# Gate weights of a gated linear recurrence get buffers of their own, gate blocks move between the recurrence's groups, and the last norm is reordered

## Chip, cores and metric

One core of one Trainium2 chip runs the whole layer in one launch. The metric is the device time of the launch in microseconds, the median of several runs. Engines are named as in the profile: PE is TensorE (PEld its weight loads), DVE is VectorE, ACT is ScalarE, POOL is GpSimd, SP is SyncE, which here issues nearly all DMAs.

## The reference, cut to what matters

The layer takes x of 256 tokens by 2048 and runs a half-step feed-forward with a norm, a mixer of two parallel branches with a norm, and a second feed-forward with a norm:

```python
h = layer_norm(DN_ALPHA * h + 0.5 * swiglu(h, ffn1_w_in, ffn1_w_out), ln1_g, ln1_b)
q, k, v, qi, ki, wi, rx, rg, gates = split_cols(h @ w_in)
y_attn = dsa_attention(q, k, v, qi, ki, wi)          # attention over the selected keys
# recurrent branch: 2560 channels in 16 blocks of 160
xc = causal_conv(rx, conv_w) + conv_b                # 4 taps
r  = sigmoid(blockdiag(xc, wa) + ba);  i = sigmoid(blockdiag(xc, wx) + bx)
a  = exp(-8 * r * softplus(-lam));     b = sqrt(1 - a*a) * (i * xc)
y_rnn = scan(h_t = a_t * h_{t-1} + b_t) * gelu(rg)
g_attn, g_rnn = split(sigmoid(gates))
merged = g_attn * (y_attn @ w_attn_branch) + g_rnn * (y_rnn @ w_rnn_branch)
h = layer_norm(DN_ALPHA * h + merged @ w_out, ln2_g, ln2_b)
h = layer_norm(DN_ALPHA * h + 0.5 * swiglu(h, ffn2_w_in, ffn2_w_out), ln3_g, ln3_b)
```

All data are float32.

## The kernel before, in words

**Products in parts.** Every float32 operand of a product is split into a high part (a rounded copy, made by ACT) and a low part (the difference, made by DVE). A product is three matmuls: high by high, low by high, high by low. For the weights the two halves of the split are the tiles `wh` (ACT, L203) and `wl` (DVE, L204), written from `raw`, the tile into which SP's DMA puts the weights.

**One stream of weights.** A list of pieces of at most 1024 columns is laid down once, in the order in which PE will use them. When PE's code comes to a new piece (`W.unit`), the load of the piece eight further is issued and the split of the piece four further. There are 4 buffers for `raw` and 5 for each of `wh` and `wl`, whatever the size of a piece. So the `raw` buffer of a new load is one whose piece DVE has just split, and the `wh`/`wl` buffer of that split is one whose piece PE has just finished.

**Order on the engines.** PE, SP and POOL run in the order in which the program is written. DVE and ACT are ordered by a scheduler at compile time, mostly by the order of writing; on the chip each engine then takes its instructions strictly in that order.

**The recurrent stage** is a loop over j from 0 to 21 (`NR` = 20 tiles of 128 channels, `LAG` = 2). For j below 20 two blocks (`blockB`, L594 and L595) project x and the gelu input of tile j; DVE and ACT sum the parts, run the convolution (L1297) and split the result into `xc`. Then, for tile i = j - 2, the gate products use 256 columns of the block-diagonal weights `lru`: `corners` for the first tile of a group, `squares` for the others (`L1247`), and `lru_gates` follows with four ACT operations (L1264 to L1267) and a reciprocal on DVE (L1268). The 20 tiles form four groups of five. At a group's last tile (i = 4, 9, 14, 19, so j = 6, 11, 16, 21) PE also runs `squares` for the group's first tile and 16 narrow matmuls (`strips`, L1254) on the weights `lx`; after that a background task `recur` does the group's square roots, products and scan, a few instructions at each new piece of the stream. `bg.drain("rec")` emits what is left of it.

**Gate blocks.** `gates(nb)`, nb = 0 to 3, multiplies x by 512 columns of the branch's output gate `wG`: 8 pieces, 96 matmuls of 512 columns, with two ACT operations (`gr`, L1278) at its end and no other work for DVE than the split of its weights. Before the change gates(0) stands at the start of j = 20, gates(1) to gates(3) after the loop. The weights `lru` are small pieces of the common stream (24 of them, 256 columns each); `lx` is loaded twice, for two groups at a time.

**The last norm** (`OuterNorm.product`, `norm`, `turned`) ends the kernel. The tokens are two halves, t = 0 and 1. For each, when the last product is in PSUM: statistics (L865, L756, L757) on DVE, the power of -0.5 on POOL (L758), then on DVE three column blocks are centred (L871) and scaled (L879) with a DMA out after each (L880), and the small factor `nm` (L875) is made for the fourth block, which ACT scales (L876), PE transposes (L887), ACT scales again (L891) and SP writes out (L892).

## Time and profile before

| what | value |
|---|---|
| median of 3 runs | 2260.11 us (2259.5 to 2261.3) |
| the profiled execution | 2260.29 us |
| its span in the profile | 2258.2 us |
| PE busy | 2236.4 us (99%) |
| DVE busy | 1956.0 us (87%) |
| ACT busy | 1445.1 us (64%) |
| recurrent stage (loop over j) | from 1061.7 to about 1321 us |
| gates(0), j = 20 | 1295.8 to 1317.9 us |
| end of the last product on PE | about 2247.7 us |

The span starts at the first instruction and ends at the last one; the profiled execution's own time has 2.1 us around it. In a row of the timeline the columns are start, duration, engine, line, operation, tiles; a bracket at the end gives the idle time of the engine before it and what ended it. A matmul of 512 columns is shown with 0.38 us, but in an unbroken row the next starts 0.22 us later, so matmuls overlap in such rows and a PE shown as busy may still have lost a little.

### The profile page before, as it was taken

The numbers are of one execution on the slowest core, as the hardware profiler recorded it, in microseconds if no ns is written. First come the engines' busy times: TensorE is split into PE (matmuls) and PEld (weight loads), VectorE is DVE, ScalarE is ACT, GpSimd is POOL, SyncE is SP. The second block draws the span as 40 slices with busy tenths as digits, with TensorE's granted clock in tenths as the row PEclk, the third lists the DMA queues.
The fourth block names the chain that finished last, engine by engine and source line by source line (L and its number), as shares of the span: only waits on it lengthen the run. The fifth ranks groups of instructions, "written<-read, shape, count | busy, mean of one in ns | idle before, by whom it ended". The sixth has DMA issues, their size and how long they took to land.

```text
span 2258.2 us, 34888 instructions
## 1 busy us (share of the span) xinstructions
PE 2236.4 (99%) x13328; PEld 2023.3 (90%) x13328; DVE 1956.0 (87%) x2743; ACT 1445.1 (64%) x2062; POOL 19.8 (1%) x54
## 2 busy tenths in 40 slices
PE   9999999999999999999999999999999999999998
PEld 8999999999988888888998888888899999999997
DVE  7999999999998776645799985656999999999997
ACT  6667777667756555544677774444766777777664
POOL 0000000000000000000000000000000000000000
PEclk9999999999999999999999999999999999999999
DMA  8555566555567655566555567666665555566554
GB/s 319 199 205 191 217 224 224 210 210 207 198 194 222 181 174 153 164 198 208 178 188 184 188 217 214 192 202 191 220 209 214 204 200 197 216 224 233 215 206 149
DMA packets 114760, 459.57 MB, mean 204 GB/s; under 512 B 12929, under 2 KB 16257, under 8 KB 100257
## 3 DMA queue, kind: packets, MB, share of 16 engines
q1 hardware_dynamic: 112176, 450.41, 59.0%
q0 software_dynamic: 1840, 5.89, 0.9%
q8 instruction: 104, 1.70, 0.3%
q10 hardware_dynamic: 576, 1.05, 0.1%
q14 instruction: 64, 0.52, 0.1%
HBM read 455.20 MB, written 2.10 MB: 203 GB/s over the span
## 4 chain that ended last, share of the span: by engine, by line
PE 87%; DVE 9%; issue 2%; ACT 1%; DMA 1%; POOL 0%; POOLq 0%; ACTq 0%; DVEq 0%
PE mm L605 11%; PE mm L607 11%; PE mm L606 11%; PE ob L605 10%; PE ob L607 10%; PE ob L606 10%; PE bp L606 4%; PE bp L607 4%; PE bp L605 4%; DVE wl L204 4%; PE mm L594 2%; PE ob L594 2%; PE mm L595 1%; PE ob L595 1%; PE bp L958 1%
## 5 line engine op out<-in xcount | busy, mean ns | idle before, releaser
L204 DVE TENSOR_TENSOR wl<-raw,wh 128x1024 fp32r<-128x1024 f32 (+2 forms) x644 | 759.8, 1185 | 239.4 <-ACT wh L203 237.1
L203 ACT ACTIVATE wh<-raw 128x1024 fp32r<-128x1024 f32 (+2 forms) x644 | 658.7, 1028 | 356.5 <-PE ob L607 138.6
L203 ACT ACTIVATE wh<-rf 128x1024 fp32r<-128x1024 f32 x336 | 301.8, 917 | 140.9 <-PE mm L607 84.9
L204 DVE TENSOR_TENSOR wl<-rf,wh 128x1024 fp32r<-128x1024 f32 x336 | 346.0, 1039 | 2.4
L605 PE MATMUL mm<-wh,hs 128*128 128x512 f32 (+1 forms) x704 | 247.3, 351 | 0.3 <-ACT hs L796 0.2
L607 PE MATMUL mm<-wh,hs 128*128 128x512 f32 (+1 forms) x704 | 244.0, 347 | 1.5 <-DVE hs L797 1.3
L605 PE MATMUL ob<-wh,g 128*128 128x512 f32 x640 | 245.5, 384 | 0.0
L606 PE MATMUL mm<-wl,hs 128*128 128x512 f32 (+1 forms) x704 | 243.6, 346 | 0.7 <-DVE wl L204 0.7
L607 PE MATMUL ob<-wh,g 128*128 128x512 f32 x640 | 242.7, 379 | 0.5 <-DVE g L737 0.5
L606 PE MATMUL ob<-wl,g 128*128 128x512 f32 x640 | 242.6, 379 | 0.0
L605 PE MATMUL bp<-wh,sh 128*128 128x256 f32 x672 | 185.0, 275 | 0.0
L606 PE MATMUL bp<-wl,sh 128*128 128x256 f32 x672 | 184.9, 275 | 0.0
L607 PE MATMUL bp<-wh,sl 128*128 128x256 f32 x672 | 184.8, 275 | 0.0
L203 ACT ACTIVATE wh<-ws 128x1024 fp32r<-128x1024 f32 x112 | 119.2, 1064 | 81.4 <-issue 52.7
L607 PEld LDWEIGHTS mm<-wh,hs 128*128 128x128 f32 x704 | 133.7, 190 | 16.1 <-DVE hs L797 3.2
L605 PE MATMUL mm<-wh,xs 128*128 128x512 f32 (+1 forms) x448 | 146.8, 328 | 0.8 <-ACT wh L203 0.8
L606 PE MATMUL mm<-wl,xs 128*128 128x512 f32 (+1 forms) x448 | 146.8, 328 | 0.5 <-DVE wl L204 0.5
L605 PEld LDWEIGHTS mm<-wh,hs 128*128 128x128 f32 x704 | 133.7, 190 | 14.7 <-issue 1.0
L607 PE MATMUL mm<-wh,xs 128*128 128x512 f32 (+1 forms) x448 | 146.5, 327 | 0.0
L606 PEld LDWEIGHTS mm<-wl,hs 128*128 128x128 f32 x704 | 133.8, 190 | 13.2 <-DVE wl L204 1.0
L176 DVE TENSOR_TENSOR ws<-rf 128x1024 f32<-128x1024 f32 x112 | 136.4, 1218 | 4.4 <-DMA rf<-f1a 2.1
L607 PEld LDWEIGHTS ob<-wh,g 128*128 128x128 f32 x640 | 121.0, 189 | 18.0 <-DVE g L737 0.9
(335 smaller groups left out, 5131.7 us busy)
## 6 DMA issues: line engine op xcount, KB each, us to landing
rf<-f1a SPq DMA_DIRECT2D x56, 1024.0 KB, 5.0
rf<-f2a SPq DMA_DIRECT2D x56, 1024.0 KB, 5.1
raw<-f1o SPq DMA_DIRECT2D x88, 512.0 KB, 5.8
raw<-f2o SPq DMA_DIRECT2D x88, 512.0 KB, 5.9
raw<-wB SPq DMA_DIRECT2D x80, 512.0 KB, 3.8
raw<-wA SPq DMA_DIRECT2D x64, 512.0 KB, 3.6
raw<-wG SPq DMA_DIRECT2D x64, 512.0 KB, 3.7
raw<-f2a SPq DMA_DIRECT2D x64, 512.0 KB, 4.6
```

The lines of the kernel that those rows point to most:

```text
L176: v.tensor_tensor(t, b[:, 0:4:3], b[:, 1:2].to_broadcast([P, 2, 2, 256]), op=OP.add)
L203: nc.scalar.activation(hp, src, AF.Copy)
L204: self.last = nc.vector.tensor_tensor(lp, src, hp, op=OP.subtract)
L594: T.matmul(ps, w[0], turns(x.rearrange("p a t -> p (a t)")), start=first, stop=False)
L595: T.matmul(ps[:, :S], w[1], turns(x[:, 0]), start=False, stop=last)
L605: T.matmul(ps, xh, h, start=start, stop=False, skip_group_check=seeded)
L606: T.matmul(ps, xh, l, start=False, stop=False, skip_group_check=seeded)
L607: T.matmul(ps, xl, h, start=False, stop=stop, skip_group_check=seeded)
L958: T.transpose(ps[:, k * S + t * P:k * S + (t + 1) * P], z[:, t * 512 + k * P:t * 512 + (k + 1) * P], ident)
```

## The change

Four edits:

- **Gate weights.** The 24 pieces of `lru` leave the common stream. A new `load_gates(i)`, called at the start of step j = i + 2, ahead of that step's two blocks where there are any, issues a DMA into a small tile `lr` and splits it into a tile `lw` of its own (ACT L733, DVE L734; line numbers of the new kernel differ from those before by up to three). Same products, same sizes.
- **`lx`** is loaded four times, once per group, into a small tile, instead of twice into a large one.
- **Gate blocks.** gates(0) goes to the start of j = 12, gates(1) to the start of j = 17, gates(2) to the start of j = 20, gates(3) after the loop.
- **Last norm.** `nm` moves from DVE to POOL; two blocks are centred before the first is scaled; and 14 products of the 128x128 identity with itself stand on PE between the transposes of t = 0 and those of t = 1.

```diff
+GR_AT = (12, 17, NR)
+WARM_END = 14
...
-    for i in range(NR + LAG):
+    for i in range(NR + 1):
+        if i in GR_AT:
+            plain([wG[4 + GR_AT.index(i)]])
         if i < NR:
             plain([wB[RX + i], wB[RG + i]])
-        if i == NR:
-            plain([wG[4]])
-        if i >= LAG:
-            g, c = divmod(i - LAG, TPG)
-            plain([lru[g][:, c * 2 * P:(c + 1) * 2 * P]])
-            if c == TPG - 1:
-                plain([lru[g][:, TPG * 2 * P:]])
-    plain(wG[4 + nb] for nb in range(1, 4))
+    plain([wG[7]])
...
                 self.turned(0)
+                warm = BP()
+                for _ in range(WARM_END):
+                    T.matmul(warm[:, :P], ident, ident, start=True, stop=True)
                 self.norm(1, ps[1], rows)
...
+            nm = SM(1)
+            G.tensor_scalar(nm, mu, r, -1.0, op0=OP.mult, op1=OP.mult)
             centered(0)
-            nm = SM(1)
-            V.tensor_scalar(nm, mu, r, -1.0, op0=OP.mult, op1=OP.mult)
+            centered(1)
             A.activation(Y[t][3], ps, AF.Identity, scale=r, bias=nm)
             for nb in range(3):
...
-                if nb < 2:
-                    centered(nb + 1)
+                if nb == 0:
+                    centered(2)
...
+    def load_gates(i):
+        g, c = divmod(i, TPG)
+        for c in (c,) if c < TPG - 1 else (c, TPG):
+            raw, hl = T1("lr"), UHL("lw")
+            nc.sync.dma_start(raw, lru[g][:, c * 2 * P:(c + 1) * 2 * P])
+            split(hl, raw)
+            lw.append([(hl[:, 0, o:o + P], hl[:, 1, o:o + P]) for o in (0, P)])
...
     for j in range(NR + LAG):
-        if j == NR:
-            gates(0)
-        if j < NR and j % (2 * TPG) == 0:
-            lx = QG("lx")
-            nc.sync.dma_start(lx, lru_x[j // (2 * TPG)])
-            lxs += [lx[:, :2 * P], lx[:, 2 * P:]]
+        if j in GR_AT:
+            gates(GR_AT.index(j))
+        if j % TPG == LAG and j < NR:
+            lxs.append(T1("lx"))
+            nc.sync.dma_start(lxs[-1], lru_x[j // TPG])
+        if j >= LAG:
+            load_gates(j - LAG)
...
-    for nb in range(1, 4):
-        gates(nb)
+    gates(3)
     hs = None
     bg.drain("rec")
```

`corners` and `squares` take their weights from `lw` instead of from the stream; nothing else in them changes.

**PE at the end of the second group (from j = 11 to 12).** The last strip matmul of the group and what follows, before:

```order
L1254 MATMUL bp_12462<-xg_12121,lx_10883 32x256
L594 MATMUL mm_12491<-hs_7425,wh_12397 128x512
L595 MATMUL mm_12491<-hs_7425,wl_12398 128x256
L594 MATMUL mm_12491<-hs_7426,wh_12397 128x512
L595 MATMUL mm_12491<-hs_7426,wl_12398 128x256
```

The same place after the change:

```order
L1254 MATMUL bp_12456<-xg_12114,lx_11762 32x256
L602 MATMUL mm_12479<-wh_12340,hs_7425 128x512
L603 MATMUL mm_12479<-wl_12341,hs_7425 128x512
L604 MATMUL mm_12479<-wh_12340,hs_7425 128x512
L602 MATMUL mm_12479<-wh_12340,hs_7426 128x512
```

Where the next block of j = 12 stood, gates(0) now begins (L602 to L604 are the three matmuls of such a block, L605 to L607 before), and the blocks of j = 12 come 96 matmuls later.

**SP around j = 20.** The DMAs of the last `lru` weights (the tiles of i = 18, of i = 19, and those of the last group's first tile) among the loads of the gate weights, before:

```order
L161 DMA raw_13599<-wG 128x1024
L161 DMA raw_13629<-wG 128x1024
L161 DMA raw_13652<-lru 128x256
L161 DMA raw_13673<-lru 128x256
L161 DMA raw_13691<-lru 128x256
L161 DMA raw_13709<-wG 128x1024
```

And after (`raw_14064` is the last piece of gates(3), whose load is issued when PE's code comes to the last piece of gates(2)):

```order
L163 DMA raw_14046<-wG 128x1024
L163 DMA raw_14064<-wG 128x1024
L1284 DMA lr_14086<-lru 128x256
L1284 DMA lr_14105<-lru 128x256
L1284 DMA lr_14110<-lru 128x256
L163 DMA raw_14153<-wrb 128x1024
```

Before, the three loads stood right behind the eight pieces of the gates(0) that PE runs ahead of them, and ahead of the eight of the next block; now they stand behind all eight of the next block.

**DVE around j = 20.** The splits of those weights, before:

```order
L204 TENSOR_TENSOR wl_13712<-raw_13629,wh_13711 128x1024
L204 TENSOR_TENSOR wl_13730<-raw_13652,wh_13729 128x256
L204 TENSOR_TENSOR wl_13748<-raw_13673,wh_13747 128x256
L204 TENSOR_TENSOR wl_13766<-raw_13691,wh_13765 128x256
L204 TENSOR_TENSOR wl_13784<-raw_13709,wh_13783 128x1024
```

And after (`wl_14067` is the fourth piece of gates(3), `wl_14156` the fifth; `vw_14097` belongs to tile i = 18):

```order
L206 TENSOR_TENSOR wl_14067<-raw_13992,wh_14066 128x1024
L206 TENSOR_TENSOR wl_14156<-raw_14010,wh_14155 128x1024
L734 TENSOR_TENSOR lw_14087<-lr_14086,lw_14087 128x256
L1268 RECIPROCAL vw_14097<-vw_14097 128x256
L734 TENSOR_TENSOR lw_14106<-lr_14105,lw_14106 128x256
L734 TENSOR_TENSOR lw_14111<-lr_14110,lw_14111 128x256
```

The second and third of the small splits now stand behind the reciprocal of tile 18, which itself needs the product of the first. On ACT they stand behind the four operations of tile 18 in the same way.

**DVE in the last norm,** from the statistics of t = 0 on, before:

```order
L757 TENSOR_SCALAR s_23053<-s_23052 128x1
L871 SCALAR_TENSOR_TENSOR y_415<-y_415,s_23052,gr_22772 128x512
L875 TENSOR_SCALAR s_23059<-s_23052,s_23054 128x1
L879 SCALAR_TENSOR_TENSOR y_415<-y_415,s_23054,br_22774 128x512
L871 SCALAR_TENSOR_TENSOR y_444<-y_444,s_23052,gr_22776 128x512
```

And after:

```order
L754 TENSOR_SCALAR s_23033<-s_23032 128x1
L871 SCALAR_TENSOR_TENSOR y_415<-y_415,s_23032,gr_22752 128x512
L871 SCALAR_TENSOR_TENSOR y_444<-y_444,s_23032,gr_22756 128x512
L880 SCALAR_TENSOR_TENSOR y_415<-y_415,s_23034,br_22754 128x512
L871 SCALAR_TENSOR_TENSOR y_475<-y_475,s_23032,gr_22760 128x512
```

The second centring takes the place of `nm`, and the scaling that needs POOL's power comes one instruction later.

More of the change, by code (lines that the diff above doesn't have):

```diff
@@ L1235, in corners @@
         banks = [BP() for _ in range(4)]
-        for gate in range(2):
-            w = W.unit(P)
+        for gate, w in enumerate(lw.popleft()):
             for n, (a, b) in enumerate(thirds(x, w)):
@@ L1244, in squares @@
     def squares(ps, x, first, last):
-        for gate in range(2):
-            for n, (a, b) in enumerate(thirds(x, W.unit(P))):
+        for gate, w in enumerate(lw.popleft()):
+            for n, (a, b) in enumerate(thirds(x, w)):
                 T.matmul(ps[:, gate * S:(gate + 1) * S], a, b, start=first and not (gate or n),
@@ L1278, in gates @@
             A.activation(gr[nb][t], ps[t], AF.Tanh, scale=0.5)
-    xgs, xcs, tiles, lxs, pairs = {}, {}, [], [], []
-    for j in range(NR + LAG):
-        if j == NR:
-            gates(0)
-        if j < NR and j % (2 * TPG) == 0:
-            lx = QG("lx")
-            nc.sync.dma_start(lx, lru_x[j // (2 * TPG)])
-            lxs += [lx[:, :2 * P], lx[:, 2 * P:]]
+    def load_gates(i):
[5 more added lines that the diff above has]
+            lw.append([(hl[:, 0, o:o + P], hl[:, 1, o:o + P]) for o in (0, P)])
+    xgs, xcs, tiles, lxs, pairs, lw = {}, {}, [], [], [], deque()
+    for j in range(NR + LAG):
+        if j in GR_AT:
[5 more added lines that the diff above has]
+            load_gates(j - LAG)
         if j < NR:
@@ L1429, in _layout @@
         wG=a_blocks(w[:, 4176 + 2 * RNN:]),
-        lru=c(np.stack(lr)), lru_x=c(np.stack([np.concatenate(lx[i:i + 2], axis=1) for i in (0, 2)])), wab=a_blocks(w_attn_branch[0]), wrb=a_blocks(regrouped(w_rnn_branch[0].T).T),
+        lru=c(np.stack(lr)), lru_x=c(np.stack(lx)), wab=a_blocks(w_attn_branch[0]), wrb=a_blocks(regrouped(w_rnn_branch[0].T).T),
         wo=a_blocks(w_out[0]), f2a=f_in(ffn2_w_in[0]), f2o=f_out(ffn2_w_out[0]), cols_d=c(cols),
```

## The prediction

> **What bounds the kernel now.** I read the page first, then PE's waits and a long window of the stage that the change touches, then its timeline.
>
> ```profile
> PE 2236.4 (99%) x13328; PEld 2023.3 (90%) x13328; DVE 1956.0 (87%) x2743; ACT 1445.1 (64%) x2062; POOL 19.8 (1%) x54
> ```
>
> PE carries the time. Since the change leaves the real matmuls as they are, only PE's pauses and the last few microseconds can move. PE's waits between 1150 and 1300 us, and the busy sums of the second and third groups of the recurrence:
>
> ```profile
> PE mm L595 <- DVE wl L204: 2.4, 3, 1.0
> PE mm L606 <- DVE wl L204: 0.7, 1, 0.7
> PE ob L595 <- DVE wl L204: 0.7, 2, 0.3
> PE mm L594 <- ACT wh L203: 0.4, 1, 0.4
> ```
>
> ```profile
> 1200.00:1300.00 100.00, 95.62 (x626) 85.11 (x626) 95.31 (x156) 78.35 (x147) 0.00 (x0) 1.00 0.58 185
> ```
>
> Here PE (95.62) and DVE (95.31 of 100 us) are both full, and PE waits for DVE's low parts. One such wait:
>
> ```profile
> 1235.00 0.38 PE L594 MATMUL mm<-hs,wh 128*128 128x512 f32 x1
> 1236.11 0.38 PE L595 MATMUL mm<-hs,wl 128*128 128x256 f32 x1 [0.73 <-DVE wl L204]
> ```
>
> The row calls 0.73 us idle, but the next matmul should have started 0.22 us after 1235.00, so 0.89 us are lost, 0.16 more than shown; the restart costs another 0.10 (the following matmul comes 0.21 us later instead of 0.11).
>
> **The change part by part. 1: the waits in the recurrence go.** The window has 100 - 95.62 = 4.4 us of idle and 3+1+2+1 = 7 waits, each hiding 0.26: 4.4 + 1.8 = 6.2 us. They come after the second and third groups, when `recur` adds its DVE work to steps that nearly fill DVE anyway. The gate blocks now stand just there: 8 splits of 1.22 us (row 1319.66 below) are 9.8 us of DVE work beside 96 matmuls at 0.216, 20.7 us of PE work, so DVE gets 11 us free, against a shortage of 6.2 us over both groups. The small pieces also no longer use up 24 of the large buffers. I take all 6.2 us as won; bounds 5 (a few tenths per group stay, since the first group's `recur` still has no gate block behind it until j = 12) and 6.2.
>
> **2: a new wait at j = 20.** This is where the order printed with the change matters. gates(2) ends on PE at a time T, and PE's next instruction is `squares` of tile 18, whose weights come from a DMA that SP issues only behind `raw_14064`. That load waits for the split of the fourth piece of gates(3), whose buffer PE frees with the next-to-last piece of gates(2). Before the change the same loads were 10 us ahead. The same point of the kernel before, at the end of its gates(0), T = 1317.88:
>
> ```profile
> 1317.84 3.40 SPq L161 DMA_DIRECT2D raw<-wG  x2
> 1319.66 1.22 DVE L204 TENSOR_TENSOR wl<-raw,wh 128x1024 fp32r<-128x1024 f32 x1 [1.85 <-ACT wh L203]
> 1317.88 0.39 PE L1247 MATMUL bp<-xc,wh 128*128 128x256 f32 x2
> 1320.98 0.48 PE L605 MATMUL ob<-wh,hs 128*128 128x512 f32 x1
> ```
>
> SP's load comes at T - 0.04; PE ran squares and strips from 1317.88 to 1320.98, 3.1 us without a wait. How long loads take: the large ones of a gate stretch, then the twelve small ones between 1190 and 1330 us, then one small one by itself, issued right behind a large load:
>
> ```profile
> L161 SPq DMA_DIRECT2D raw<-wrb x7: 327/328/328, 1365.6 to 1380.6; - x7
> ...
> DMA to landing us min/median/max: 3.9/4.4/4.5
> ```
>
> ```profile
> L161 SPq DMA_DIRECT2D raw<-lru x12: 327/328/328, 1196.6 to 1310.1; - x12
> ...
> DMA to landing us min/median/max: 2.0/2.1/4.6
> ```
>
> ```profile
> L161 SPq DMA_DIRECT2D raw<-lru x1: 328/328/328, 1258.1 to 1258.1; - x1
> ...
> DMA to landing us min/median/max: 3.7/3.7/3.7
> ```
>
> A small load alone takes 2.1 us; behind a large one it took 3.7, and at most 4.6. So: large load at T, small one issued at T + 0.35 (SP's 0.33 for one), landing with or just after the large one at about T + 4.5 (large median 4.4). Then the durations of the small split, the four ACT operations and the reciprocal:
>
> ```profile
> L203 ACT ACTIVATE wh<-raw 128x256 fp32r<-128x256 f32 x14 | 5.6, 412 | 3.1 <-DMA raw<-lru 1.7 <-PE mm L607 1.4
> L204 DVE TENSOR_TENSOR wl<-raw,wh 128x256 fp32r<-128x256 f32 x14 | 5.4, 397 | 1.6 <-ACT wh L203 1.4
> L1268 DVE RECIPROCAL vw<-vw 128x256 f32<-128x256 f32 x13 | 22.6, 1744 | 1.9 <-ACT vw L1267 1.9
> ```
>
> ```profile
> 1321.98 0.48 ACT L1264 ACTIVATE t<-bp,hba 128x256 f32<-128x256 f32 x1
> 1322.69 0.62 ACT L1266 ACTIVATE vw<-t,sp 128x256 f32<-128x256 f32 x1
> 1324.13 0.43 ACT L1267 ACTIVATE vw<-vw 128x256 f32<-128x256 f32 x1
> ```
>
> First wait: ACT's half at T + 4.94, DVE's at T + 5.4 (0.41 + 0.40 and some hundredths); the four matmuls that need it finish at T + 6.0. Second wait: the split for tile 19 is queued behind tile 18's operations on both engines. From the end of tile 18's product: L1264 to L1266 0.71, L1266 0.62, L1267 0.43, then the reciprocal 1.74, then the split 0.40: 3.9 us until PE can go on. Then 0.45 us for the rest of tile 19, 0.67 for the first tile, 1.0 for the strips: gates(3) starts at T + 6.0 + 6.0 = T + 12.0 instead of T + 3.1. Cost 8.9 us. Nothing else is lost there: five pieces of gates(3) are split by then, 13 us of PE work.
>
> Bounds: if the small load landed 2.1 us after its issue, the split would still stand behind the large one of DVE (1319.66 + 1.22, that is T + 3.0), so the first wait ends at T + 3.4 and the cost is 6.9 us. That is the floor, as the second wait stands whatever the DMA does. The other steps' loads (j up to 19) are issued 10 us before use, against 4.5 us to land: nothing.
>
> **3: PE's clock in that wait.** At the end of the kernel PE pauses for 3.83 us, and the rows after it are slow:
>
> ```profile
> 2247.50 0.60 PE L887 MATMUL bp<-ident,y 128*128 128x128 f32 x4
> 2251.93 1.12 PE L887 MATMUL bp<-ident,y 128*128 128x128 f32 x4 [3.83 <-ACT y L876]
> 2252.00:2253.00 1.00, 1.00 (x4) 0.65 (x4) 0.96 (x2) 0.00 (x0) 0.00 (x0) 0.50 0.46 176
> ```
>
> Granted clock 0.50, and the same four transposes take 1.12 us instead of 0.60. The new first wait is about 5 us, longer than that, and the second nearly as long, so I expect half clock when PE goes on. How long it lasts, only the start of the program bounds:
>
> ```profile
> L401 PE MATMUL bp<-tri x20: 421/421/581, 1.0 to 5.2; 128*128 128x128 f32 x20
> 7.50 0.38 PE L607 MATMUL mm<-wh,xs 128*128 128x512 f32 x1
> ```
>
> 20 passes in 4.2 us are 0.21 each, the slow pace; at 7.50 the pace is 0.22 for four times the columns. So half clock lasts 4.2 to 6.5 us of activity and costs half of that, 2.1 to 3.2; nothing if the clock isn't lowered. I take 2.1.
>
> [...]
>
> **4: the tail.** Rows of the last norm:
>
> ```profile
> 2243.63 0.74 DVE L871 SCALAR_TENSOR_TENSOR y<-y,s,gr 128x512 f32<-128x512 f32 x1
> 2248.51 0.69 DVE L865 BATCH_NORM_STATS2 st<-mm 128x6 f32<-128x512 f32 x1
> 2249.77 0.99 POOL L758 TENSOR_TENSOR s<-s,mhalf 128x1 f32<-128x1 f32 x1 [4.98 <-DVE s L757]
> 2250.79 0.21 DVE L875 TENSOR_SCALAR s<-s,s 128x1 f32<-128x1 f32 x1 [0.44 <-POOL s L758]
> 2251.10 0.78 ACT L876 ACTIVATE y<-mm,s,s 128x512 f32<-128x512 f32 x1 [1.46 <-DVE s L875]
> 2253.09 1.50 ACT L891 ACTIVATE o<-bp,cols 128x128 f32<-128x128 f32 x4 [1.21 <-PE bp L887]
> 2251.69 3.23 SPq L880 DMA_DIRECT2D out<-y  x3
> 2255.01 0.38 SPq L892 DMA_DIRECT2D out<-o  x1
> ```
>
> DVE holds back t = 1: its statistics start at 2248.51, when the work of t = 0 is done. Without the wait for POOL, six blocks at a pitch of 0.67 from 2243.63 end at 2247.65, as PE does. That is 0.8 us earlier. POOL's power for t = 1 then ends at 2249.96. The new POOL operation has no row; the nearest are a fill of one column (0.10) and the power itself (0.99). I take 0.6, between them, for a two-input multiply. ACT starts at 2250.64 (before: 2251.10), the transposes 0.83 later, and take 0.60, since the 14 identity products (28 passes of 0.11 at full clock, 3.0 us) end at 2250.9 and lie inside the pause. ACT's four finish at 2253.6, and the last DMA goes out at 2253.65 instead of 2255.01, no longer behind the third block's. Gain 1.4 us; bounds 1.0 (POOL 0.99) and 1.8 (0.10).
>
> Two more ACT table loads and the four small `lx` loads lie on engines with room (ACT 78 of 100 us above): nothing.
>
> **Sum.** -6.2 + 8.9 + 2.1 - 1.4 = +3.4 us. The profiled execution took 2260.29 us (span 2258.2), 0.2 above the median 2260.11, so I predict 2263.5. The terms' ends: low -6.2 + 6.9 + 0 - 1.8 = -1.1 (2259.0), high -5 + 8.9 + 3.2 - 1.0 = +6.1 (2266.2).
>
> **The rivals.** *Small loads overtake.* The small load lands 2.1 us after its issue, like the median of the twelve, though a large one is ahead of it; the first wait is then 3.4 us, below the 3.83 that lowered the clock. -6.2 + 6.9 + 0 - 1.4 = -0.7, 2259.4. Against it stands the small load of 1258.1 with its 3.7 us. [...]
>
> *The new wait is not there* (faster): SP's small loads are early enough after all, because ACT and DVE run ahead of what the order suggests, and the reciprocal is done before PE asks. Then -7.6 us, 2252.5. It needs the first wait under 1 us and the second, too; against it speaks that `raw_14064` needs a buffer that PE frees 2.6 us before T, and that the reciprocal needs tile 18's product. From a cost of 3.1 us downwards it decides for faster.
>
> *Slow clock lasts* (slower): the two pauses each lower the clock, and gates(3) runs its first 6.5 us of activity at half: with tile 18's product slowed by 0.5, -6.2 + 9.4 + 3.2 - 1.4 = +5.0, 2265.1. It decides above 12.1 us of cost at j = 20.
>
> *The gate blocks don't cure the DVE shortage:* half of the 6.2 us stays; +6.5, 2266.6. DVE's 11 free microseconds speak against it.
>
> **How the numbers follow.** A change of 0.2%, 4.5 us, is about what a measurement of this kernel can tell from none. Forecast 0.48, overtaking loads 0.14 (both within 0.2%), wait absent 0.14 (faster), slow clock 0.16 and shortage 0.08 (slower). Within 0.2%: 0.62 of these, of which I give 0.02 to the slower side for the forecast's own upper end. The forecast's own range is 2259 to 2266; leaving out most of the faster case and little above gives 2256.5 to 2267.
>
> **What would show it.** In the profile after: no waits of PE for `wl` between j = 12 and 19; two waits of `bp` matmuls (`squares`) at j = 20 and 21, for the small ACT or DVE split, about 5 and 3.9 us, right after a gate block; granted clock under 1.00 there; the transposes of t = 1 at 0.60 us; DVE's last statistics right behind PE's last matmul. Wrong it would be if those two waits are short, or if DVE's shortage shows at j = 10 to 19 as before.

## The result: 0.5% slower, and the profile after

| what | before | after |
|---|---|---|
| median of 4 runs | 2260.03 us | 2271.90 us (2271.04 to 2273.15) |
| ratio | | 1.0052, 95% interval 1.0035 to 1.0070 |
| the profiled execution | 2260.29 us | 2272.62 us |
| its span | 2258.2 us | 2270.8 us |
| recurrent stage: first matmul of j = 0 to first matmul of the branch product that follows gates(3) | 1061.69 to 1383.25: 321.6 us | 1061.33 to 1396.89: 335.6 us |
| last product matmul to the end of the span | 11.0 us | 10.1 us |

The forecast was 2263.5 us with a range up to 2267.0. The time lies 4.9 us above that range. In the two profiles the stage grew by 14.0 us, the time ahead of it shrank by 0.36 and the time behind it by 1.05: 12.6 us, the difference of the spans. So the stage holds it all.

The page's first line says nothing of it: PE is at 99% as before. The list of PE's waits between 1190 and 1400 us does. Its columns are total, number, longest:

```profile
PE bp L1247 <- ACT lw L733: 9.0, 3, 6.4
PE bp L1247 <- DVE lw L734: 1.3, 2, 1.0
PE bp L1241 <- ACT lw L733: 1.1, 2, 0.6
PE ob L591 <- ACT gr L1278: 1.0, 1, 1.0
PE mm L591 <- ACT gr L1278: 0.7, 1, 0.7
PE mm L602 <- DVE t L724: 0.3, 1, 0.3
```

No line for `wl` is left: the waits of before, which the change was forecast to remove, are gone. In their place stand waits for the small weights `lw` and for PSUM banks that the Tanh of a gate block (`gr`) still holds. The busy sums of two stretches of 100 us show where they are (columns behind the length: PE, PEld, DVE, ACT, POOL, granted clock, which is the share of its full clock at which PE may run, DMA share, GB/s):

```profile
1200.00:1300.00 100.00, 97.88 (x567) 86.19 (x567) 85.03 (x126) 71.64 (x128) 0.00 (x0) 1.00 0.57 188
1300.00:1400.00 100.00, 88.59 (x479) 76.66 (x478) 73.92 (x106) 64.38 (x104) 0.00 (x0) 0.93 0.55 176
```

In the first DVE fell from 95 to 85 of 100 us, and yet PE still stands for 2.1 us. In the second PE stands for 11.4 us and the granted clock is below 1. Most of that is j = 20, with 9.5 us in three waits; PE's rows there:

```profile
1358.95 0.38 PE L604 MATMUL mm<-wh,hs 128*128 128x512 f32 x1
1365.74 1.68 PE L1247 MATMUL bp<-xc,lw 128*128 128x256 f32 x6 [6.42 <-ACT lw L733]
1369.59 0.80 PE L1247 MATMUL bp<-xc,lw 128*128 128x256 f32 x2 [2.17 <-ACT lw L733]
1371.35 2.50 PE L1247 MATMUL bp<-xc,lw 128*128 128x256 f32 x10 [0.96 <-DVE lw L734]
1373.79 1.94 PE L1254 MATMUL bp<-xg,lx 128*32 128x256 f32 x16
1375.65 0.80 PE L602 MATMUL ob<-wh,hs 128*128 128x512 f32 x1
```

gates(2) ends at T = 1359.17 (the last row of it plus its 0.22), gates(3) starts at 1375.65: 16.5 us where the kernel before took 3.1. The wait is the one that the forecast described, larger. Its causes stand in the rows of SP, ACT and DVE at that place:

```profile
1354.50 4.95 SPq L163 DMA_DIRECT2D raw<-wG  x3
1359.50 1.38 SPq L1284 DMA_DIRECT2D lr<-lru  x3
...
1365.28 0.42 ACT L733 ACTIVATE lw<-lr 128x256 fp32r<-128x256 f32 x1 [4.37 <-DMA lr<-lru]
...
1369.27 1.75 DVE L1268 RECIPROCAL vw<-vw 128x256 f32<-128x256 f32 x1 [3.12 <-ACT vw L1267]
1370.94 0.69 DVE L734 TENSOR_TENSOR lw<-lr,lw 128x256 fp32r<-128x256 f32 x2
```

The small load is issued at T + 0.33 and its split starts at T + 6.1; then tile 19's split on DVE stands behind tile 18's reciprocal, as forecast. That the small loads are late not only here is shown by the view of the tile `lr` between 1200 and 1370 us:

```profile
L1284 SPq DMA_DIRECT2D lr<-lru x12: 423/426/642, 1228.1 to 1360.4; - x12
...
  DMA lr<-lru: 18.0, 8
...
DMA to landing us min/median/max: 2.7/4.7/5.8
```

The middle line is the idle time of the engines that use the tile: 8 of the 12 times ACT came to the split first and stood, 18.0 us in all, with everything behind it in ACT's order standing too. The first of these loads, at j = 12 behind gates(0), in the rows of SP, ACT and PE:

```profile
1226.42 1.61 SPq L1294 DMA_DIRECT2D lx<-lru_x  x1
1228.08 0.43 SPq L1284 DMA_DIRECT2D lr<-lru  x1
1230.82 0.42 ACT L733 ACTIVATE lw<-lr 128x256 fp32r<-128x256 f32 x1 [3.31 <-DMA lr<-lru]
1231.29 1.18 PE L1241 MATMUL bp<-xc,lw 32*128 32x256 f32 x24 [0.60 <-ACT lw L733]
```

SP sends the load off at 1228.08, 2.4 us before PE comes to its product (1230.5).

The end of the kernel, to be held against the rows of before:

```profile
2261.19 0.70 DVE L865 BATCH_NORM_STATS2 st<-mm 128x6 f32<-128x512 f32 x1
2263.54 0.87 POOL L874 TENSOR_SCALAR s<-s,s 128x1 f32<-128x1 f32 x1
2265.28 0.66 PE L888 MATMUL bp<-ident,y 128*128 128x128 f32 x4 [0.56 <-ACT y L877]
```

The statistics now start 0.42 us after the last product matmul (2260.77) starts, instead of 1.22; the transposes take 0.66 instead of 1.12.

### The profile page after: what moved, and what is told of

Its sections match the earlier page's. It is cut to its first block, busy times and chain, and to the rows that moved or that the text cites. A ratio compares the mean times of both kernels' runs of the same rounds, so it can differ in the third digit from the quotient of the medians.

```text
span 2270.8 us, 34937 instructions
## 1 busy us (share of the span) xinstructions
PE 2243.1 (99%) x13356; PEld 2028.7 (89%) x13356; DVE 1958.4 (86%) x2741; ACT 1449.3 (64%) x2064; POOL 21.6 (1%) x56
## 3 DMA queue, kind: packets, MB, share of 16 engines
q10 hardware_dynamic: 576, 1.05, 0.1%
## 4 chain that ended last, share of the span: by engine, by line
PE 84%; DVE 9%; issue 2%; ACT 2%; DMA 2%; SPq 0%; POOL 0%; ACTq 0%; POOLq 0%; DVEq 0%
PE mm L602 11%; PE mm L604 11%; PE mm L603 11%; PE ob L602 10%; PE ob L604 10%; PE ob L603 10%; DVE wl L206 4%; PE bp L604 4%; PE bp L603 4%; PE bp L602 4%; PE ob L591 2%; DMA lr<-lru 2%; PE mm L591 1%; PE ob L592 1%; PE bp L959 1%
## 5 line engine op out<-in xcount | busy, mean ns | idle before, releaser
L206 DVE TENSOR_TENSOR wl<-raw,wh 128x1024 fp32r<-128x1024 f32 (+1 forms) x620 | 751.5, 1217 | 217.1 <-ACT wh L205 214.3
L205 ACT ACTIVATE wh<-raw 128x1024 fp32r<-128x1024 f32 (+1 forms) x620 | 648.9, 1052 | 335.1 <-PE ob L604 131.2
L602 PE MATMUL mm<-wh,hs 128*128 128x512 f32 (+1 forms) x704 | 247.4, 351 | 0.5 <-DVE t L724 0.3
L604 PE MATMUL mm<-wh,hs 128*128 128x512 f32 (+1 forms) x704 | 244.0, 347 | 1.5 <-DVE hs L794 1.3
L602 PE MATMUL ob<-wh,g 128*128 128x512 f32 x640 | 245.5, 384 | 0.0
L604 PE MATMUL ob<-wh,g 128*128 128x512 f32 x640 | 242.7, 379 | 0.5 <-DVE g L734 0.5
L602 PE MATMUL bp<-wh,sh 128*128 128x256 f32 x672 | 185.0, 275 | 0.0
L604 PE MATMUL bp<-wh,sl 128*128 128x256 f32 x672 | 184.8, 275 | 0.0
L604 PEld LDWEIGHTS mm<-wh,hs 128*128 128x128 f32 x704 | 133.7, 190 | 16.2 <-DVE hs L794 3.1
L602 PE MATMUL mm<-wh,xs 128*128 128x512 f32 (+1 forms) x448 | 146.8, 328 | 1.1 <-ACT wh L205 1.1
L602 PEld LDWEIGHTS mm<-wh,hs 128*128 128x128 f32 x704 | 133.7, 190 | 15.3 <-issue 1.4
L604 PE MATMUL mm<-wh,xs 128*128 128x512 f32 (+1 forms) x448 | 146.5, 327 | 0.0
L206 DVE TENSOR_TENSOR wl<-ws,wh 128x1024 fp32r<-128x1024 f32 x112 | 136.0, 1215 | 1.2 <-ACT wh L205 1.0
```

Source lines behind the costliest of these rows:

```text
L205: nc.scalar.activation(hp, src, AF.Copy)
L206: self.last = nc.vector.tensor_tensor(lp, src, hp, op=OP.subtract)
L602: T.matmul(ps, xh, h, start=start, stop=False, skip_group_check=seeded)
L604: T.matmul(ps, xl, h, start=False, stop=stop, skip_group_check=seeded)
```

## The experiments

Times are medians; the kernel before, run beside each group, took 2260.67, 2260.49 and 2260.58 us. "Stage" is the stage of the table above, read from each trace in the same way; it is cut further into the part from gates(0)'s to gates(2)'s first matmul (j = 12 to 19) and the part from there to the end of gates(3).

| kernel | time | ratio to before | stage | j = 12 to 19 | gates(2) to end of gates(3) |
|---|---|---|---|---|---|
| before | 2260.03 | 1 | 321.6 | | |
| after | 2271.90 | 1.0052 (1.0035 to 1.0070) | 335.6 | 139.65 | 59.03 |
| two loads early | 2259.77 | 0.9997 (0.9988 to 1.0005) | 321.9 | 138.97 | 45.51 |
| all loads early | 2255.84 | 0.9977 (0.9968 to 0.9986) | 316.8 | 135.22 | 44.65 |
| blocks only | 2253.86 | 0.9970 (0.9959 to 0.9981) | 315.1 | 133.40 | 44.65 |
| first wait filled | 2271.79 | 1.0051 (1.0037 to 1.0064) | 334.0 | 138.00 | 57.70 |
| last norm only | 2259.78 | 0.9996 (0.9987 to 1.0005) | 321.1 | | |
| buffers only | 2267.66 | 1.0032 (1.0020 to 1.0043) | 327.8 | | |
| small loads on POOL's queue | 2259.99 | 0.9996 (0.9987 to 1.0005) | 322.5 | 133.39 | 52.18 |
| blocks and last norm | 2252.67 | 0.9964 (0.9952 to 0.9977) | 315.1 | 133.43 | 44.65 |
| both waits filled | 2270.72 | 1.0043 (1.0029 to 1.0056) | 332.9 | 139.14 | 55.50 |
| the same, `nm` on DVE | 2254.14 | 0.9971 (0.9959 to 0.9982) | 315.1 | 133.40 | 44.64 |
| POOL's queue and early | 2252.37 | 0.9964 (0.9951 to 0.9976) | 314.9 | 133.40 | 44.65 |
| blocks and last norm, no identity products | 2253.07 | 0.9966 (0.9954 to 0.9979) | 315.2 | 133.50 | 44.65 |

("The same" in the line for `nm` is the kernel of blocks and last norm.) Five and six kernels give 133.4 and 44.65 us for the two parts to 0.1 us: that is what they take without a wait, and against it each cost is read.

### Two loads early

```diff
+        if j == NR:
+            load_gates(NR - 2)
+            load_gates(NR - 1)
         if j in GR_AT:
             gates(GR_AT.index(j))
...
-        if j >= LAG:
+        if LAG <= j < NR:
             load_gates(j - LAG)
```

> The changed kernel with one move: the weights of tiles 18 and 19 (three loads of 128 KB, their splits) are asked for ahead of gates(2) instead of behind it; all else as in the changed kernel (2271.9 us). Theory: of the 11.8 us lost, 13.4 come from the stretch between the end of gates(2) and the start of gates(3) (16.5 us instead of 3.1), because these loads are issued there and land 5.75 us later. They now have 20 us: the stretch falls to about 3.1 us and the time to 2258.5 (2257.5 to 2260). Rival 1, the excess sits elsewhere (in the steps j = 12 to 19 that the gate blocks now split): no more than 5 us come back, 2267 or more. Rival 2, the wait moves: the three loads stand ahead of the pieces of gates(2) in SP's queue and gates(2) starves by what they gain, 2265 to 2272.

Measured: 2259.77 us. The last part fell from 59.03 to 45.51 us, and PE's waits from 1190 to 1400 us are down to these:

```profile
PE bp L1241 <- ACT lw L733: 1.8, 2, 1.6
PE mm L591 <- ACT gr L1278: 1.0, 1, 1.0
PE mm L602 <- DVE t L724: 0.6, 1, 0.6
```

Three loads asked for one gate block earlier bring back 12.1 us of the median, 13.5 in the profile: the place of these three loads costs what the change loses. Neither rival holds: gates(2) does not starve. The part j = 12 to 19 still takes 5.6 us more than without waits; some of that is slow clock, which in this trace was at half from 1233.9 to 1237.3 us, after the wait of 1.6 us.

### All loads early

```diff
+        if j >= LAG - 1 and j <= NR:
+            load_gates(j - LAG + 1)
         if j in GR_AT:
             gates(GR_AT.index(j))
...
-        if j >= LAG:
-            load_gates(j - LAG)
```

> The changed kernel, but every step asks for its small gate weights one step earlier and ahead of that step's gate block. Theory: besides the 13.4 us at j = 20 the waits of the corners and squares for the small splits at j = 12 to 19 go too (0.76, 0.49, 0.71, 0.32 and 0.69 us, 3.0 in all), since the loads then have about 10 us more: 2255.5 (2254 to 2257.5), and PE's waits for lw vanish from the profile. What stays are the waits for the bank that the two Tanh of a gate block hold, about 2 us. Rival: the small waits come from DVE and ACT being full, not from late loads; then earlier loads change nothing at j = 12 to 19 and the time equals that of the kernel with two loads early, about 2258.5.

Measured: 2255.84 us, as the theory had it; the part j = 12 to 19 takes 135.22 us, 1.8 more than without waits. PE's list, and from the view of the loads' line (1190 to 1370 us) who waited for them:

```profile
PE mm L591 <- ACT gr L1278: 0.9, 1, 0.9
PE ob L591 <- ACT gr L1278: 0.2, 1, 0.2
```

```profile
  ACT lw L733: 7.1, 6
```

The waits for `lw` are gone, so they came from late loads and not from full engines, the rival. ACT still stands 7.1 us, 6 times, before small splits (18.0 in the changed kernel), and the waits for the `gr` banks, which ACT frees, remain.

### Blocks only

Against the kernel before:

```diff
     for i in range(NR + LAG):
+        if i in GR_AT:
+            plain([wG[4 + GR_AT.index(i)]])
         if i < NR:
             plain([wB[RX + i], wB[RG + i]])
-        if i == NR:
-            plain([wG[4]])
...
-    plain(wG[4 + nb] for nb in range(1, 4))
+    plain([wG[7]])
```

> The kernel before with one part of the change alone: gates(0), gates(1), gates(2) at j = 12, 17, 20, in the loop and in the weight stream; the small gate weights stay in the weight stream, as they were, and the last norm too. Theory: the waits for wl after the second and third group (6.2 us) go, because DVE gets 11 us free in each gate block; two waits for the bank behind a gate block come (2 us); no wait at j = 20, since the stream runs 8 pieces ahead: 2255.9 (2254.5 to 2257.5). Rival: it was not the blocks but the buffers that ended the waits for wl (24 small pieces no longer take large buffers and no longer turn the step of the background work): then the waits for wl stay here, 2260 to 2262.

Measured: 2253.86 us, 2 us less than expected: the bank waits do not come either. PE's list is empty, and in the stretch in which it lost 4.4 us before it loses nothing:

```profile
1200.00:1300.00 100.00, 100.00 (x587) 89.54 (x587) 91.47 (x137) 78.26 (x134) 0.00 (x0) 1.00 0.64 207
```

The stage is 6.5 us shorter than before. So the gate blocks between the groups do all of the good, and buffers of their own are not needed for it.

### Buffers only

Against "all loads early":

```diff
-GR_AT = (12, 17, NR)
+GR_AT = (NR,)
...
-    gates(3)
+    for nb in range(1, 4):
+        gates(nb)
```

> The changed kernel with the loads one step earlier, but with the gate blocks where the kernel before had them: gates(0) at j = 20, the other three behind the loop. So buffers of their own for the small gate weights, without blocks between the groups. Theory: DVE is short of time after the second and third groups, and separate buffers do not change that: PE waits for wl, 5 to 6 us between j = 10 and j = 20, and the time is about 2261 (2259.5 to 2262.5), 5 to 6 us above the kernel with all loads early (2255.8). Rival: the 24 small pieces that no longer take a large buffer, nor a step of the background work, are enough: no waits for wl, 2255 to 2257, and blocks or buffers would each do.

Measured: 2267.66 us, 6.7 us more than the theory said. The waits for `wl` are there, as it said, 4.9 us in 7:

```profile
PE mm L592 <- DVE wl L206: 3.8, 5, 1.6
PE mm L602 <- DVE t L724: 3.8, 1, 3.8
PE ob L592 <- DVE wl L206: 1.1, 2, 0.6
```

That settles blocks against buffers. The second line was not expected: gates(0) waits 3.8 us for its second bank, which DVE's sum (`t`) of j = 19's block still holds. In DVE's order that sum, at 1303.04, stands behind a reciprocal, a small and two large splits and a piece of `recur`.

### Small loads on POOL's queue

```diff
-            nc.sync.dma_start(raw, lru[g][:, c * 2 * P:(c + 1) * 2 * P])
+            nc.gpsimd.dma_start(raw, lru[g][:, c * 2 * P:(c + 1) * 2 * P])
```

> The changed kernel with one word changed: the small gate weights' loads are issued on POOL's queue instead of SP's, at the same place in the program. POOL has nothing else to do there, so a load starts when its buffer comes free and stands behind no large load. Theory: what made the loads late is their place in SP's queue, behind a large load that waits for a split: nearly all of the 13.4 us at j = 20 and of the 3.0 us at j = 12 to 19 come back: 2256 to 2259. Rival 1: what made them late is the load on the DMA engines or the buffer's release, whichever queue issues: the first wait at j = 20 stays over 4 us, 2267 to 2272. Rival 2: the loads come early, but ACT's and DVE's order still puts the second split behind the first tile's chain: the second wait of 3.9 us stays and the slow clock with it, 2261 to 2264.

Measured: 2259.99 us, between the theory's range and that of rival 2, and this run splits the cost in the same way. From 1200 to 1300 us PE is shown busy all the time; not a wait is left at j = 12 to 19, neither for `lw` nor for a `gr` bank. At j = 20 the first wait is gone and the second stays:

```profile
1353.09 0.83 PE L1247 MATMUL bp<-xc,lw 128*128 128x256 f32 x6
1356.85 0.49 PE L1247 MATMUL bp<-xc,lw 128*128 128x256 f32 x2 [2.93 <-ACT lw L733]
1358.61 2.50 PE L1247 MATMUL bp<-xc,lw 128*128 128x256 f32 x10 [1.27 <-DVE lw L734]
```

So SP's queue made the loads late; the order of ACT and DVE makes the second wait whatever the loads do (rival 2), and it costs 7.5 us in the last part, slow clock included: near the forecast's floor of 6.9, which rested on this second wait.

The two DMA lists of the seconds after T also show why the first wait was longer than forecast. The last large load ahead of the small ones, in the changed kernel (1359 to 1366 us), with the small ones behind it, and here (1352 to 1359 us), without them; the last column is the median time to landing:

```profile
raw<-wG SPq DMA_DIRECT2D x1, 512.0 KB, 5.8
...
lr<-lru SPq DMA_DIRECT2D x3, 128.0 KB, 5.6
```

```profile
raw<-wG SPq DMA_DIRECT2D x1, 512.0 KB, 4.4
```

The same load takes 4.4 us alone and 5.8 with three small ones right behind it, and these land 0.35 us and more after it. That the large ones ahead of it followed each other more closely there (1.9 us instead of 2.6) is not the reason: with two loads early they did so at 1.6 us, without small ones behind, and the load took 4.6. The 1.4 us are not a fixed price, though: with two loads early another large load, with the same three small ones right behind it (1342.22 us), landed after 4.9 us, and they after 4.6 to 4.9. What POOL's queue saved is not the time of issuing (0.54 us for one on POOL, 0.43 on SP), but the place in SP's order, behind large loads that wait for a buffer.

### Both cures

Against "all loads early":

```diff
-            nc.sync.dma_start(raw, lru[g][:, c * 2 * P:(c + 1) * 2 * P])
+            nc.gpsimd.dma_start(raw, lru[g][:, c * 2 * P:(c + 1) * 2 * P])
```

> The changed kernel with both cures: small loads on POOL's queue and one step earlier, ahead of the gate block. Theory: POOL's queue took away all waits at j = 12 to 19, the earlier step the second wait at j = 20 (a split queued behind tile 18's chain); together nothing is left of the change's cost and its blocks and last norm bring what they bring in the best kernel: 2252.7 to 2254, no waits in PE's list between j = 10 and 21. Rival: the waits for the bank that the Tanh of a gate block hold stay (1.1 and 0.4 us with the loads one step earlier on SP's queue): 2255.5.

Measured: 2252.37 us and an empty list of PE's waits; from 1200 to 1300 us PE is shown busy all the time. So in the recurrent stage the buffers themselves cost nothing once their loads are asked for in time; the whole loss there was the order of loads and splits. (The end of the kernel is 0.4 us longer with them, see the last norm below.) That the `gr` waits went too, which stayed when the loads had the same lead on SP's queue, ties them to ACT's standing before small splits; which instruction of ACT held them up each time was not followed further.

### The clock: one wait filled, then both

Against the changed kernel; the first run has `j == NR` and 24, the second is as shown:

```diff
+                if j >= NR:
+                    fill = BP()
+                    for _ in range(24 if j == NR else 12):
+                        T.matmul(fill[:, :P], ident, ident, start=True, stop=True)
                 squares(banks[c - 1], xcs[i], False, True)
```

> The changed kernel with 24 products of the identity with itself (48 passes of 0.117 us, 5.6 us) put into a bank of their own ahead of the squares of j = 20: the loads are as late as before, but PE is not idle in the first wait. It parts the 13.4 us at j = 20 into wait and clock. Theory: the granted clock stays at full speed through tiles 18 and 19, and what the slow clock cost there comes back: six matmuls took 1.68 instead of 0.67 us, ten 2.50 instead of 1.12, the strips 1.94 instead of 1.07, together 3.3 us: 2268.6 (2267.5 to 2269.5). Rival 1, the clock's share is the 2.1 us of the forecast or less: 2269.8 to 2271. Rival 2, the slow matmuls run beside waits that would be there anyway: 2271.9.

Measured with one wait filled: 2271.79 us, the forecast's gain missed. The clock did not stay up (columns as above; the 0.50 third from last is the granted clock):

```profile
1368.00:1374.00 6.00, 3.40 (x16) 2.88 (x20) 2.36 (x3) 3.18 (x8) 0.00 (x0) 0.50 0.00 0
```

Tile 18's six matmuls ran at full clock (1.00 from 1366.0 to 1367.5; 1.17 instead of 1.68 us, waits included), but 0.4 us into the second wait, at 1367.85, the clock was halved, and tile 19 was as slow as before. So this run alone could not part clock and wait; the second one was made for that:

> The changed kernel with identity products in both waits of j = 20 and 21: 24 ahead of tile 18's squares and 12 (24 passes, 2.8 us at full clock) ahead of tile 19's. With the first wait alone filled the granted clock fell again 0.4 us into the second wait, and the ten matmuls of tile 19 still took 2.50 us; so the clock's share is not parted from the wait's yet. Theory: with both filled the clock stays at full speed, the loads stay late, and the stretch from the end of gates(2) to gates(3) falls from 16.5 us to 13.3, by 1.0 (tile 18's six matmuls), 1.4 (the ten) and 0.9 (the strips): 2269 beside a kernel before of 2260.5 (2268 to 2270). Rival: the slow matmuls are not on the path, the fills only push work back: 2271 to 2273.

```profile
1362.22 5.52 PE L1327 MATMUL bp<-ident 128*128 128x128 f32 x48
1368.14 1.17 PE L1247 MATMUL bp<-xc,lw 128*128 128x256 f32 x6 [0.40 <-ACT lw L733]
...
1373.24 1.38 PE L1247 MATMUL bp<-xc,lw 128*128 128x256 f32 x10 [1.03 <-DVE lw L734]
1374.55 1.07 PE L1254 MATMUL bp<-xg,lx 128*32 128x256 f32 x16
```

Here the clock stays at 1.00, the ten matmuls take 1.38 instead of 2.50 us and the strips 1.07 instead of 1.94. gates(3) starts at 1375.55, 13.3 us after gates(2)'s end at 1362.2, as expected, but in part by luck. From gates(2) to the end of gates(3) it takes 55.50 us instead of 59.03; of these 3.5 us some 0.6 come from a first wait that happened to be shorter (resumed after 5.92 us instead of 6.57); the rest, 2.9, is the clock's, 0.4 of it in the first matmuls of gates(3). The median moved less, to 2270.72, between the two ranges: in this kernel, as in the one before it, 1.4 us were lost ahead of j = 12, 1.0 of them by small waits of the squares of j = 9 to 11, and its interval overlaps that of the changed kernel. The size of the clock's share thus rests on the traces, not on the medians.

### The last norm by itself, and its parts

Against the kernel before:

```diff
                 self.turned(0)
+                warm = BP()
+                for _ in range(WARM_END):
+                    T.matmul(warm[:, :P], ident, ident, start=True, stop=True)
                 self.norm(1, ps[1], rows)
...
+            G.tensor_scalar(nm, mu, r, -1.0, op0=OP.mult, op1=OP.mult)
             centered(0)
-            V.tensor_scalar(nm, mu, r, -1.0, op0=OP.mult, op1=OP.mult)
+            centered(1)
```

> The kernel before with the third part of the change alone: the last norm reordered and 14 identity products ahead of its second transposes. Theory: from PE's last product matmul to the end of the span it takes 10.03 us in the changed kernel instead of 10.91, so 0.9 us are gained: 0.9 us under the kernel before in the span (2257.3 instead of 2258.2 plus or minus what two profiles differ by), a median of about 2259.8 beside 2260.7, too little for the interval to part it from no change. Rival, the forecast's 1.4 us: the span ends 9.5 us after the last product matmul; then POOL's multiplication cannot be the 0.87 us that the changed kernel's profile shows.

Measured: 2259.78 us, no difference that the interval shows. In the trace the last product matmul starts at 2246.96 and the span ends at 2256.65: 9.7 us, against 10.96 before; that is nearer to the rival's 9.5 than to the theory's 10.03, with POOL's multiplication still at 0.87 us. The last DMA is issued 6.73 us after that matmul, in the changed kernel too, instead of 7.72, and lands in 2.00 instead of 2.27 us, no longer right behind another one: 1.26 us together. The changed kernel's profile shows 0.4 us less, because 1.34 us pass between that landing and its end instead of 0.96. So it is in every trace with the small tiles and in none without them. At the end SP waits for the semaphores (counters) of the DMAs one after another, 0.06 us each: with the small tiles six more of these waits stand behind that of the last DMA (seven in the changed kernel, from 2269.59 to 2269.95, one in the kernel before). No run changes this order by itself.

Without the identity products, against "blocks and last norm":

```diff
-                warm = BP()
-                for _ in range(WARM_END):
-                    T.matmul(warm[:, :P], ident, ident, start=True, stop=True)
```

> The best kernel so far (2252.7) without the 14 identity products ahead of the second transposes. Theory: PE is idle for about 3.7 us there, the granted clock falls to 0.50 and the four transposes take 1.12 us instead of 0.66; the span ends 0.45 us later, the median at 2253.1, which the interval can't part. Rival: the reordered norm makes the pause too short for the clock to fall, and the transposes stay at 0.6 us: 2252.7, and the products were worth nothing.

Measured: 2253.07 us, and

```profile
2245.32 0.66 PE L890 MATMUL bp<-ident,y 128*128 128x128 f32 x4 [3.68 <-ACT y L879]
2246.50:2247.00 0.50, 0.00 (x0) 0.00 (x0) 0.00 (x0) 0.50 (x2) 0.00 (x0) 0.79 0.79 299
```

In this execution the outcome is the rival's: after 3.68 us of idle PE the clock is still full, the four transposes take the same 0.66 us, and from the last product matmul to the end it takes 9.70 us with and without the products. But the rival's reason does not hold. The pause was not too short: the second row's 0.79 says that the clock was halved at 2246.79, 0.8 us after the transposes had ended and 5.2 us after the last matmul ahead of the pause. In the kernel before it was halved 3.4 us after it, and in "blocks only" 4.0 us, each time in time to slow the transposes (1.12 and 1.01 us). Why it came later in this execution no run shows. The medians, 2253.07 and 2252.67, fit the theory's 0.45 us as well as none, so whether the products are worth anything is not shown.

With `nm` on DVE, against "blocks and last norm" (and 12 identity products instead of 14):

```diff
-            G.tensor_scalar(nm, mu, r, -1.0, op0=OP.mult, op1=OP.mult)
             centered(0)
+            V.tensor_scalar(nm, mu, r, -1.0, op0=OP.mult, op1=OP.mult)
             centered(1)
```

> The best kernel so far (blocks in the stream, reordered last norm; 2252.7) with the product of mean and reciprocal deviation put back on DVE, between the first two blocks' operations, and 12 identity products instead of 14. It measures the term of the forecast that had no row, POOL's multiplication. Theory: POOL's 0.87 us and its start 0.1 us behind the power are on the path; DVE's 0.21 us take their place, at most 0.2 us late behind a block's 0.74: from the last product matmul to the end of the span it takes 0.4 to 0.7 us less than the 9.7 us of that kernel, and the transposes stay at 0.66 us or less; the median 2252.1, too near to be told apart. Rival: DVE's third block ends later and its out DMA then ends the span: no gain in the span.

Measured: 2254.14 us, and 10.5 us from the last product matmul to the end, 0.8 more. Counted from the last product matmul the transposes started only 0.1 us earlier (4.39 instead of 4.51 us behind it), and SP's rows show what then bound the end:

```profile
2245.23 2.32 SPq L886 DMA_DIRECT2D out<-y  x3
2247.65 0.40 SPq L898 DMA_DIRECT2D out<-o  x1
```

DVE waits for POOL's power before `nm` (0.44 us), its three blocks end 1.2 us later (6.8 instead of 5.6 us behind that matmul), and the last DMA now stands right behind theirs in SP's queue; with POOL's multiplication SP was free for 0.8 us between them. The 0.87 us on POOL that looked like a loss keep DVE free. So the rival held, and the end came later, not earlier.

### Blocks and last norm

Against "blocks only", the last norm as in "the last norm by itself":

```diff
+            G.tensor_scalar(nm, mu, r, -1.0, op0=OP.mult, op1=OP.mult)
             centered(0)
-            V.tensor_scalar(nm, mu, r, -1.0, op0=OP.mult, op1=OP.mult)
+            centered(1)
...
```

> The version that the runs point to: gate blocks at j = 12, 17 and 20 with the small weights left in the weight stream, and the reordered last norm, so the change without its buffers. Theory: the gains add up, 6.8 us of the blocks (2253.9 beside 2260.7) and 0.9 of the last norm: 2253.0 (2252 to 2254). Rival: in that kernel the end is bound by something else (the third block's out DMA), and the last norm adds nothing: 2253.9.

Measured: 2252.67 us, 0.36% under the kernel before (0.9964, interval 0.9952 to 0.9977): the change without its buffers, the fastest together with "both cures" (2252.37, the same ratio). The gains add up as expected.

## Why the prediction was wrong, step by step

**Step 1, the waits in the recurrence (-6.2): right in itself.** With the blocks alone the stage shrinks by 6.5 us, and without the blocks the `wl` waits stay, so the reason given, DVE's time, stands.

**The step that failed: the small loads of j = 12 to 19, put at nothing.** It is the sentence at the end of step 2: "The other steps' loads (j up to 19) are issued 10 us before use, against 4.5 us to land: nothing." They are not issued when PE begins the step. SP takes its DMAs in order, and ahead of a small load stand large ones that wait for a buffer: the small load of the first one after gates(0) went out at 1228.1, for a product that PE had reached at 1230.5, so 2.4 us ahead and not 10. Right ahead of it SP had also spent 1.61 us on issuing the load of `lx` (0.4 us at the other three groups), a term that the forecast put at nothing too; no run tests it apart. Waits for `lw`, and for banks that ACT freed late, cost 139.65 - 133.40 = 6.25 us, as much as step 1 had won. With the loads on POOL's queue this term is zero.

**Steps 2 and 3, the new wait at j = 20 (+8.9) and its clock (+2.1): the mechanism right, the size too small.** 59.03 - 44.65 = 14.4 us stand against 11.0. The stretch from T to gates(3) was forecast as 6.0 to the end of tile 18's product, 3.9 for the chain, 2.1 for the rest and 2.1 for the clock, 14.1. Measured: 8.0, 4.15 and 4.3, the slow matmuls within them. Two terms were mis-sized. In the first the small load landed 5.75 us after its issue instead of some 4.2: the large one ahead of it took 5.8 us instead of 4.4, and the small one landed behind it. That small loads right behind it lengthen a large one was seen at this place and, by less (4.9), in one other; what sets the amount stays open. The remaining half microsecond of the first term is slow clock. The second is the clock's share: 2.9, within its bounds of 0 to 3.2 but not the 2.1 taken. Its source was weak: for the 20 passes at the start of the program the profile's column of the granted clock reads 1.00, so those rows show a slow pace but no lowered clock. Two losses outside that stretch were not in the sum: a bank wait of 0.6 us in gates(2), and gates(3)'s first matmuls at half clock, 0.4 (part of the 2.9).

**Step 4, the last norm (-1.4): right, 1.26 up to the landing of the last DMA,** of which the changed kernel's profile shows 0.9 at its end, 0.4 being lost in SP's last waits. That the number came so near is luck in part: POOL's multiplication took 0.87 us, near the bound of 0.99 and not the 0.6 taken, and the 0.27 us of the shorter landing, which was not in the sum, made up for it. The transposes took 0.66 us, near the 0.60 that the forecast had from the identity products; but without these they took the same in the one trace there is, in which the clock fell late, so that what the products gave is not shown.

**Sum in the profile.** -6.5 + 6.25 + 14.4 - 0.9 = +13.25; the difference of the spans is 12.6. The remaining -0.7 us lie outside the steps: 0.36 ahead of the stage, 0.16 in its first two groups, 0.16 between the stage and the last norm. Forecast: +3.4.

**The rivals.** *Small loads overtake:* no, they landed 0.35 us and more behind the large one. *The new wait is not there:* no. *Slow clock lasts:* partly; the clock was at half until 1376.5 us, through both waits, but it cost 2.9 us where the forecast had 2.1 in its sum, the small part of a miss of 8.4. *The blocks don't cure the shortage:* no, they cure all of it. The case that happened was none of these: small loads late at the steps before j = 20 too. It was left out because the waits of the kernel before, which had the same loads eight pieces ahead in the stream, could not show it, and the order of SP, which does, was read only around j = 20.

## What to carry to other kernels

A load that leaves a look-ahead stream for a buffer of its own loses its lead: its time of issue is then set by the queue in which it stands, in program order behind loads that wait for buffers (here the first one after gates(0) went out 2.4 us ahead of its product). Give it the lead back (ask one step earlier) or a queue that nothing blocks: the one gave back 16 us here, the other 12, and both together the whole cost of 20. When a step of a forecast says "issued early enough: nothing", look up in that queue what stands ahead of it, and what stands behind the instruction that will wait for it on an engine that runs in order. And test the parts of a change apart: here one part won 6.5 us, one about 1, and the third, needed by neither, lost 20.

## What the runs showed of the hardware

- Where a trace shows the granted clock fall and rise again, it stayed at half for 3.41 us (two loads early, 1233.91 to 1237.33), 6.83 us (first wait filled, 1367.85 to 1374.68; POOL's queue, 1357.76 to 1364.59) or 13.65 us (changed kernel, 1362.87 to 1376.53). The moments follow from the granted clock of windows of half a microsecond.
- In these traces the length of a pause alone does not tell when the clock falls. It fell 3.5 us after the last matmul in the changed kernel's first wait, and 3.4, 4.0 and 5.2 us after it in pauses of 3.7 to 3.8 us at the end of three kernels (the kernel before, blocks only, no identity products). In the first two of these it slowed the matmuls behind the pause, in the third it did not.
- Nor did PE stand long before every fall. With the first wait filled the clock fell at 1367.85, 0.4 us after tile 18's six matmuls had ended; with POOL's queue it fell at 1357.76, 0.4 us after a pair of matmuls had ended, which followed a wait of 2.93 us.
- Once halved, the clock came back 5.2 us after PE had gone on without a pause in the changed kernel (1371.35 to 1376.5), 3.3 us with the first wait filled (1371.4 to 1374.7) and 6.0 us with POOL's queue (1358.6 to 1364.6).
- Three loads of 128 KB right behind one of 512 KB landed after it both times that the traces were read for it; the large one took 5.8 us in the changed kernel and 4.9 with two loads early, against 4.4 and 4.6 without small ones behind it.
- In the last norm a multiplication of a column of 128 values on POOL takes 0.87 us, almost what its power takes there (0.98); the same power took 0.55 us in the norm behind the recurrent stage.
